# The fullest expert's 96 slots as three products of 32 columns instead of 64 + 32

## The chip, the core and the metric

The kernel runs on one core of a Trainium2 chip. The metric is the device time of one execution in microseconds: 2082.15 us is the median of three runs before the change (2079.93 to 2087.93). One further execution was profiled, and all rows below come from it.

## What is computed

The reference is a two-layer backbone block for a diffusion generator: 256 latent and 256 context tokens of width 1024. Layer 0 mixes the sequence with a bidirectional state-space scan, layer 1 with bidirectional retention. Each layer ends in a mixture of 32 experts, of which every token takes two from one group of eight. This part is what the change touches:

```python
def expert_block(args):
    xb, e = args
    gu = xb @ w_gate_up[e]                       # 1024 -> 2 x 512
    return (jax.nn.silu(gu[:, :MOE_HIDDEN]) * gu[:, MOE_HIDDEN:]) @ w_down[e]   # 512 -> 1024
...
return jnp.sum(out[dest].reshape(n_tok, MOE_TOP_K, -1) * top_w[..., None], axis=1)
```

Layer 0 routes 512 tokens (context and latent), layer 1 the 256 latent ones. All arithmetic is in f32.

## The kernel before

**Slots and places.** The router sorts the experts by their number of tokens (a few by fixed position), and the table `SLOTS` gives each position a number of slots, 32, 64 or 96. One position per layer, number 4, has 96. `MoE.__init__` puts positions together into *places* of 128 slots: two experts of 64, four of 32, or the *full* place, which is position 4 (96 slots) and one partner with 32. Layer 0 has twelve places, of which the full one is the fourth; layer 1 has ten, and it is the second.

**One place.** The tokens of a place's slots stand in `xT` as eight slabs of 128 features by 128 slots. `gate_up` (L1810) runs over eight slabs `k`, and in each over two halves: gate into the PSUM bank `pg`, up into `pu`. In every half each expert multiplies: its slot columns of `xT` are the stationary operand (so an expert with 32 slots uses 32 columns of TensorE's array and 32 partitions of the result), and 512 columns of its weights stream through. `hidden_T` turns the activated result (L1827, `ph`), `down` (L1839) does four slabs of two halves in the same way into `pd`, `weighted` scales and splits it, and `add` brings it back to the tokens with a one-hot matrix (L1857, `pc`; L1882 and L1883 on VectorE). I call one half of one slab a *step*: a place has 16 gate/up steps and 8 down steps, whatever its kind. Which products a step has is set by `tiles_of` (L1501): a list of pairs (expert, width), used by `pairs`, by `gate_up` and `down` through `parts`, and by `slot_w` (L1769), where VectorE reduces one row per tile.

For the full place `tiles_of` gives widths 64, 32 and 32: the expert at position 4 multiplies twice per step, with slots 0 to 63 on columns 0 to 63 and slots 64 to 95 on columns 64 to 95, both times with the same streamed weights; the partner has columns 96 to 127.

**The one-hot rows.** `scatter_oh` (L1780) spreads each tile's token positions over its columns with a small bf16 product per tile (`pb`), all with the same streamed operand `posT`. It compares them with a column of slot numbers, which `pairs` picks by the widths: 0 to 31 repeated for four experts, 0 to 63 repeated for two, 0 to 95 for the full place.

**The weight stream.** An expert's weights are six loads of 1 MB: four for gate and up (two slabs each), two for down. The ring (`Ring`) issues all loads of both layers in one order from SP's queue (L175): place by place, and within a place load 0 of each expert, then load 1. It has 16 slots of 1 MB in layer 0 and 19 in layer 1, in five kinds named A, B, E, F and X. A load waits in SP's queue until the product that last read its slot is done, and all loads behind it wait too.

**The order on TensorE.** The program is written place by place, but a scheduler orders each engine's instructions. It mixes gatherings of a later place (`px`, L1749), the one-hot sums (`pc`) and weights (`pw`) into the steps, and it may move the partner's products away from those of position 4. What it has placed is fixed when the kernel is built.

Of the kernel before, what the change touches and what calls it, by code (L numbers as in the profile page):

```python
# [198 lines left out]
def col(S, name, a=0, b=None):  # L199
    o, w = CL[name]  # L200
    return S.c[:, o + a:o + (w if b is None else b)]
# [1272 lines left out]
class MoE:  # L1474
# [25 lines left out]

    def tiles_of(self, places):  # L1501

        return [(e, w) for e in places for w in ([64, 32] if self.slots(e) == 96 else [self.slots(e)])]

    def slots(self, e):
        return SLOTS[self.layer][e]
# [379 lines left out]
    def pairs(self):  # L1886
        S, order, groups = self.S, self.order, self.groups
        i96, s32, s64, s96 = (col(S, n) for n in ("i96", "s32", "s64", "s96"))
        xT, ws, G = {}, {}, self.G
        last = len(order) - 1  # L1890

        def one_hots(g):
            runs = []
            for e in (e for p in groups[g] for e in order[p]):
                if runs and e == runs[-1][1] and self.slots(e) == self.slots(runs[-1][0]):
                    runs[-1][1] += 1
                else:
                    runs.append([e, e + 1])
            return self.gather_oh([(self.pos[:, :, a:b], self.slots(a)) for a, b in runs], i96)

        def weights(g):
            for j, p in enumerate(groups[g]):
                ws[p] = self.slot_w(G[g], P * j, order[p])

        def start(g):
            for p in groups[g]:
                xT[p] = self.wk.tile([P, 8, P], F32, name="xT", bufs=3)

        def part(g, q, nb=2):
            self.gather(G[g], [xT[p] for p in groups[g]], q, nb)  # L1910

        def ahead(p, g):
            own = groups[g - 1]
            for q in range(4)[slice(4 * own.index(p) // len(own), 4 * (own.index(p) + 1) // len(own))]:
                part(g, q)
            if p == own[-1]:
                weights(g)
        start(0)
        prev = None
        later = self.rest_of_route()  # L1920

        def first(k):
            if k < 2 or k % 2 == 0:
                part(0, k if k < 2 else k // 2, 1 if k < 2 else 2)
            if k in ROUTE_K:
                next(later)

        def after(th, W, os_, w, end=False):
            nonlocal prev
            hT = self.hidden_T(th)  # L1930
            if prev is not None:
                self.add(*prev)
            pd = self.down(W, hT)
            prev = (os_, pd, w) if end else (os_, self.weighted(pd, w), 2)
        for p, places in enumerate(order):
            g = next(j for j, own in enumerate(groups) if p in own) + 1
            new = g < len(groups) and p == groups[g - 1][0]
            experts = {e: Expert(S, self.layer, e) for e in places}
            tiles = self.tiles_of(places)
            W = [(experts[e], w) for e, w in tiles]  # L1940
            if new and p:
                G[g] = one_hots(g)
            th = self.gate_up(W, xT[p], None if p else first)
            if p == 0:
                G[1] = one_hots(1)
                self.spread_rows()
            widths = [w for _, w in tiles]
            os_ = self.scatter_oh([(S.id2[:, e:e + 1], w) for e, w in tiles],
                                  s32 if widths[0] == 32 else s64 if widths[1] == 64 else s96)
            if g < len(groups):  # L1950
                if p == 0:
                    weights(0)
                    self.blocks()
                    self.base()
                if new:
                    start(g)
                if p > LATE:
                    ahead(p, g)
            after(th, W, os_, ws[p], p == last)
            if g < len(groups) and p <= LATE:  # L1960
                ahead(p, g)
            if p == REST[self.layer]:
                self.add(*prev)
                prev = None
                self.rest()
        return prev
# [287 lines left out]
```

## Time and profile before

| what | value |
|---|---|
| median of three runs | 2082.15 us |
| profiled execution, own time | 2085.92 us |
| its span, first to last instruction | 2084.1 us |
| granted TensorE clock, mean | 0.950 |
| first mixer (0 to 648 us) | PE busy 553.52, stream 144 GB/s |
| experts of layer 0 (648 to 1190) | PE busy 506.01, stream 363 GB/s |
| retention (1190 to 1584) | PE busy 337.07, stream 174 GB/s |
| experts of layer 1 (1584 to 2084) | PE busy 432.36, stream 371 GB/s |

Times count from the span's start. The *stream* is what the DMA engines moved, nearly all of it weights. In the two expert stages both TensorE and the stream are busy most of the time, so which of them a stretch waits for has to be read from that stretch. A row such as `pg<-ringB,xT 128*64 128x512` is a product that writes `pg`, with a stationary operand of 128 by 64 from `xT` and 512 streamed columns of a weight slot of kind B. The timeline joins instructions that follow one another, and names a joined row by its first one.

### The profile page before, as it was taken

The numbers are of one execution on the slowest core, as the hardware profiler recorded it, in microseconds if no ns is written. First come the engines' busy times: TensorE is split into PE (matmuls) and PEld (weight loads), VectorE is DVE, ScalarE is ACT, GpSimd is POOL, SyncE is SP. The second block draws the span as 40 slices with busy tenths as digits, with TensorE's granted clock in tenths as the row PEclk, the third lists the DMA queues.
The fourth block names the chain that finished last, engine by engine and source line by source line (L and its number), as shares of the span: only waits on it lengthen the run. The fifth ranks groups of instructions, "written<-read, shape, count | busy, mean of one in ns | idle before, by whom it ended". The sixth has DMA issues, their size and how long they took to land. (4 is left out here: it accounts for less than half of the span.)

```text
span 2084.1 us, 24190 instructions
## 1 busy us (share of the span) xinstructions
PE 1829.0 (88%) x9251; PEld 1038.1 (50%) x9251; DVE 1010.0 (48%) x1755; ACT 503.8 (24%) x879; POOL 517.6 (25%) x332
## 2 busy tenths in 40 slices
PE   7798889889986999999998879888897999878886
PEld 4576657567674432333332368776873233223221
DVE  3868687877576432251432475664444333103112
ACT  2655454554212100000000143232232001000000
POOL 1454645454335000000000053364551100000000
PEclk9899999999996999999999989999997999999999
DMA  7332322234845997699998844455467969999996
GB/s 292 109 122 81 129 104 101 102 131 151 282 156 202 365 395 310 249 417 382 414 403 352 333 162 162 165 199 176 130 237 299 409 253 409 409 378 407 409 409 254
DMA packets 137947, 544.42 MB, mean 261 GB/s; under 512 B 10369, under 2 KB 10881, under 8 KB 125153
## 3 DMA queue, kind: packets, MB, share of 16 engines
q1 hardware_dynamic: 137392, 542.59, 67.8%
q8 instruction: 75, 1.23, 0.2%
q14 instruction: 48, 0.39, 0.1%
q10 hardware_dynamic: 432, 0.21, 0.0%
HBM read 537.52 MB, written 5.24 MB: 260 GB/s over the span
## 5 line engine op out<-in xcount | busy, mean ns | idle before, releaser
L430 POOL TENSOR_TENSOR wl<-ringA,wh 128x1024 fp32r<-128x1024 f32 x117 | 295.3, 2539 | 808.2 <-ACT wh L429 800.4
L429 ACT ACTIVATE wh<-ringA 128x1024 fp32r<-128x1024 f32 x120 | 126.1, 1058 | 193.5 <-issue 45.3
L1839 PE MATMUL pd<-ringB,hT 128*32 128x512 f32 (+1 forms) x448 | 143.2, 640 | 5.8 <-ACT hT L1829 4.1
L1850 DVE SCALAR_TENSOR_TENSOR yh<-pd,ws,yh 128x512 fp32r<-128x512 f32 x40 | 30.0, 751 | 206.5 <-ACT yh L1849 204.9
L1819 DVE SCALAR_TENSOR_TENSOR th<-th,pg 128x512 f32<-128x512 f32 x22 | 15.1, 687 | 222.5 <-ACT th L1815 222.5
L1815 ACT ACTIVATE th<-pg 128x512 f32<-128x512 f32 x22 | 13.1, 597 | 432.7 <-PE pg L1810 422.6
L1810 PE MATMUL pg<-ringE,xT 128*32 128x512 f32 (+1 forms) x308 | 110.8, 611 | 7.9 <-DMA ringE<-in_moe_w_gate_up_dram 7.4
L2114 POOL TENSOR_TENSOR oacc<-oacc,ringX 128x512 f32<-128x512 f32 x1 | 1.6, 1623 | 452.2 <-ACT oacc L196 452.2
L1810 PE MATMUL pu<-ringE,xT 128*32 128x512 f32 (+1 forms) x308 | 111.0, 615 | 2.5 <-DMA ringE<-in_moe_w_gate_up_dram 2.5
L1882 DVE TENSOR_TENSOR tl<-pc,ringB 128x512 f32<-128x512 f32 x124 | 80.9, 685 | 44.6 <-PE pc L1857 43.0
L1810 PE MATMUL pg<-ringB,xT 128*32 128x512 f32 (+1 forms) x260 | 94.5, 620 | 7.2 <-DMA ringB<-in_moe_w_gate_up_dram 7.2
L1173 PE MATMUL pin<-u,wh 128*128 128x256 f32 (+1 forms) x256 | 84.1, 329 | 16.7 <-DVE gT L1225 11.3
L726 DVE SCALAR_TENSOR_TENSOR cacc<-pad,cw,cacc 128x512 f32<-128x512 f32 x96 | 94.5, 987 | 7.0 <-ACT cacc L724 6.3
L1810 PE MATMUL pu<-ringB,xT 128*32 128x512 f32 (+1 forms) x260 | 93.7, 616 | 0.1
L1810 PE MATMUL pg<-ringA,xT 128*32 128x512 f32 (+1 forms) x232 | 87.1, 603 | 6.4 <-DMA ringA<-in_moe_w_gate_up_dram 5.9
L1749 PEld LDWEIGHTS px<-oh,hhl 128*128 128x128 f32 x576 | 73.3, 193 | 35.6 <-issue 33.2
L1857 PE MATMUL pc<-yh,os 128*128 128x512 f32 x248 | 82.5, 432 | 8.5 <-DVE tl L1882 8.0
L1810 PE MATMUL pu<-ringA,xT 128*32 128x512 f32 (+1 forms) x232 | 86.4, 608 | 1.8 <-DMA ringA<-in_moe_w_gate_up_dram 1.8
L1839 PE MATMUL pd<-ringE,hT 128*32 128x512 f32 (+1 forms) x232 | 80.9, 614 | 7.4 <-DMA ringE<-in_moe_w_down_dram 4.5
L969 POOL TENSOR_TENSOR cd<-cb,tokv 128x512 f32<-128x512 f32 x64 | 73.2, 1144 | 46.2 <-DVE W L973 25.4
L1749 PE MATMUL px<-oh,hhl 128*128 128x256 f32 (+1 forms) x576 | 83.2, 294 | 0.0
L1174 PE MATMUL pin<-u,wh 128*128 128x256 f32 (+1 forms) x256 | 82.5, 322 | 0.1
(403 smaller groups left out, 4326.4 us busy)
## 6 DMA issues: line engine op xcount, KB each, us to landing
ringE<-in_moe_w_gate_up_dram SPq DMA_DIRECT2D x76, 1024.0 KB, 18.0
ringB<-in_moe_w_gate_up_dram SPq DMA_DIRECT2D x63, 1024.0 KB, 16.6
ringA<-in_moe_w_gate_up_dram SPq DMA_DIRECT2D x55, 1024.0 KB, 15.1
ringB<-in_moe_w_down_dram SPq DMA_DIRECT2D x53, 1024.0 KB, 18.0
ringA<-in_mod_w_dram SPq DMA_DIRECT2D x40, 1024.0 KB, 5.0
ringF<-in_moe_w_gate_up_dram SPq DMA_DIRECT2D x34, 1024.0 KB, 17.6
ringX<-in_moe_w_gate_up_dram SPq DMA_DIRECT2D x28, 1024.0 KB, 17.4
ringE<-in_moe_w_down_dram SPq DMA_DIRECT2D x28, 1024.0 KB, 18.1
```

Source lines behind the costliest of these rows:

```text
L429: S.split = nc.scalar.activation(hi, w, AF.Copy).ins
L430: (eng or nc.gpsimd).tensor_tensor(lo, w, hi.bitcast(F32), OP.subtract)
L726: nc.vector.scalar_tensor_tensor(acc, pad[:, :, t:t + 256], cw[:, m, t:t + 1], acc, op0=OP.mult, op1=OP.add)
L969: G.tensor_tensor(cd[d], cb[:, d, c, None, :].to_broadcast([P, 4, 128]), tokv[:, c, 0, o:o + 4, None].to_broadcast([P, 4, 128]), OP.mult)
L1173: self.S.nc.tensor.matmul(p, a, self.uh(k)[:, T], start=k == 0, stop=False)
L1174: self.S.nc.tensor.matmul(p, a, self.ul(k)[:, T], start=False, stop=False)
L1749: nc.tensor.matmul(px[:, b, :], self.S.hhl[i][:, m, j * 128:(j + 1) * 128], oh[:, i], start=i == 0 and m == 0, stop=i == nt - 1 and m == 1)
L1810: nc.tensor.matmul(po[o:o + n, :], xT[:, k, a:a + n], w.get(k)[:, u * 512:(u + 1) * 512], start=k == 0, stop=k == 7)
L1839: nc.tensor.matmul(pd[u % n][o:o + m, :], hT[:, j, a:a + m], w.get(8 + j)[:, u * 512:(u + 1) * 512], start=j == 0, stop=j == 3)
L1850: self.S.nc.vector.scalar_tensor_tensor(yl[:, u], p, ws, yh[:, u].bitcast(F32), op0=OP.mult, op1=OP.subtract)
L1857: self.S.nc.tensor.matmul(pc, os_[s, i * 128:(i + 1) * 128], ys[q][s, u % n], start=q == 0, stop=q == 1)
L1882: V.tensor_tensor(t, pc, self.gate(i)[:, c], OP.mult)
```

## The change

For the full place, the expert at position 4 gets three tiles of 32 slots where it had one of 64 and one of 32. With the partner, a step then has four products of 32 columns. Since the first width is now 32 in this place too, the choice of the slot-number column is made by the number of experts.

```diff
     def tiles_of(self, places):
-        return [(e, w) for e in places for w in ([64, 32] if self.slots(e) == 96 else [self.slots(e)])]
+
+        return [(e, w) for e in places for w in ([32] * 3 if self.slots(e) == 96 else [self.slots(e)])]
...
             os_ = self.scatter_oh([(S.id2[:, e:e + 1], w) for e, w in tiles],
-                                  s32 if widths[0] == 32 else s64 if widths[1] == 64 else s96)
+                                  s64 if widths[0] == 64 else s32 if len(experts) == 4 else s96)
```

The numbers of slots, the grouping into places, the order of the loads and the results are the same. From L1503 on, lines move down by one.

On TensorE, the end of the gate/up steps of layer 0's full place, before (`ringB` is a slot with weights; rows of 64 and of 32 columns belong to position 4, a single row of 32 at the start of a pair to the partner):

```order
L1810 MATMUL pg<-ringB,xT 64x512
L1810 MATMUL pg<-ringB,xT 32x512
L1810 MATMUL pu<-ringB,xT 64x512
L1810 MATMUL pu<-ringB,xT 32x512
L1810 MATMUL pg<-ringB,xT 32x512
L1810 MATMUL pu<-ringB,xT 32x512
L1810 MATMUL pg<-ringB,xT 64x512
L1810 MATMUL pg<-ringB,xT 32x512 x2
L1810 MATMUL pu<-ringB,xT 64x512
L1810 MATMUL pu<-ringB,xT 32x512 x2
L1827 MATMUL ph<-c,th 128x128 x4
```

And the same stretch after the change:

```order
L1811 MATMUL pg<-ringB,xT 32x512 x3
L1811 MATMUL pu<-ringB,xT 32x512 x3
L1811 MATMUL pg<-ringB,xT 32x512
L1811 MATMUL pu<-ringB,xT 32x512
L1811 MATMUL pg<-ringB,xT 32x512 x4
L1811 MATMUL pu<-ringB,xT 32x512 x4
L1828 MATMUL ph<-c,th 128x128 x4
```

Nothing changes its place: each pair 64 and 32 becomes three of 32, and where the partner stood apart it still does.

On TensorE, the end of the down steps of the same place, before (`px` is the gathering for a later place, `ringX` a slot with the partner's weights):

```order
L1749 MATMUL px<-oh,hhl 128x256 x11
L1839 MATMUL pd<-ringX,hT 32x512 x2
L1839 MATMUL pd<-ringB,hT 64x512
L1839 MATMUL pd<-ringB,hT 32x512
L1839 MATMUL pd<-ringX,hT 32x512
L1839 MATMUL pd<-ringB,hT 64x512
L1839 MATMUL pd<-ringB,hT 32x512
L1839 MATMUL pd<-ringX,hT 32x512
L1749 MATMUL px<-oh,hhl 128x256 x7
```

After the change:

```order
L1750 MATMUL px<-oh,hhl 128x256 x11
L1840 MATMUL pd<-ringX,hT 32x512 x2
L1840 MATMUL pd<-ringB,hT 32x512 x3
L1840 MATMUL pd<-ringX,hT 32x512
L1840 MATMUL pd<-ringB,hT 32x512 x3
L1840 MATMUL pd<-ringX,hT 32x512
L1750 MATMUL px<-oh,hhl 128x256 x8
```

Again the products stay where they were; one product of a gathering moved behind the last down step.

On TensorE, the first gate/up steps of layer 1's full place, before:

```order
L1810 MATMUL pu<-ringX,xT 32x512 x2
L1810 MATMUL pg<-ringX,xT 64x512
L1810 MATMUL pg<-ringX,xT 32x512 x2
L1810 MATMUL pu<-ringX,xT 64x512
L1810 MATMUL pu<-ringX,xT 32x512 x2
L1810 MATMUL pg<-ringA,xT 64x512
```

After the change:

```order
L1811 MATMUL pu<-ringX,xT 32x512 x3
L1811 MATMUL pg<-ringX,xT 32x512 x4
L1811 MATMUL pu<-ringX,xT 32x512 x4
L1811 MATMUL pg<-ringA,xT 32x512 x4
```

Here the partner's product stands in the same row as the three others in nearly every step. SP's, ScalarE's and GpSimd's instructions keep their order; on VectorE the full place has one more reduction in `slot_w`, and a few additions near it trade places.

## Prediction

> **What bounds the kernel now.** I read the page first, for the engines' shares and for the slices of the whole span.
>
> ```profile
> PE 1829.0 (88%) x9251; PEld 1038.1 (50%) x9251; DVE 1010.0 (48%) x1755; ACT 503.8 (24%) x879; POOL 517.6 (25%) x332
> ...
> DMA  7332322234845997699998844455467969999996
> GB/s 292 109 122 81 129 104 101 102 131 151 282 156 202 365 395 310 249 417 382 414 403 352 333 162 162 165 199 176 130 237 299 409 253 409 409 378 407 409 409 254
> ```
>
> TensorE is busy nearly everywhere, so its share says little by itself. The slices of 52.1 us say more: in the two expert stages (slices 13 to 22 and 31 to 39) the weight stream runs at 380 to 417 GB/s, with one hole in each, slices 15 and 16 (310 and 249) and slice 32 (253). I looked up what runs there: it is the one place per layer that the change touches. The busy time of the gate and up products (L1810) and then of the down products (L1839), by stretch, gives its price. The columns are the stretch, its length, PE busy (records), PEld busy (records), the clock, the DMA share and GB/s.
>
> ```profile
> 783.00:826.00 43.00, 37.38 (x96) 6.47 (x96) 1.00 0.80 314
> ...
> 851.00:875.00 24.00, 17.76 (x128) 5.81 (x128) 1.00 0.71 268
> ...
> 1629.00:1667.00 38.00, 33.85 (x96) 5.70 (x96) 1.00 1.03 409
> ...
> 1690.00:1713.00 23.00, 17.76 (x128) 5.80 (x128) 1.00 0.71 268
> ```
>
> ```profile
> 826.00:851.00 25.00, 19.80 (x48) 3.37 (x48) 1.00 0.44 166
> ...
> 875.00:894.00 19.00, 10.88 (x64) 2.86 (x64) 1.00 1.02 414
> ...
> 1667.00:1690.00 23.00, 17.91 (x48) 3.02 (x48) 1.00 0.52 196
> ...
> 1713.00:1733.00 20.00, 12.52 (x64) 3.15 (x64) 0.91 1.03 408
> ```
>
> The first and third rows of each fence are the full place of layer 0 and of layer 1, the second and fourth the place of four experts right behind it. Both kinds have 16 gate/up steps and 8 down steps. The place of four issues more records (128 against 96) and takes half the time. The reason stands in the timeline of PE: start, length, instructions.
>
> ```profile
> 820.55 2.05 PE L1810 MATMUL pg<-ringB,xT 128*64 128x512 f32 x6
> ...
> 821.55 1.05 PE L1810 MATMUL pg<-ringB,xT 128*32 128x512 f32 x4
> 822.53 2.05 PE L1810 MATMUL pu<-ringB,xT 128*64 128x512 f32 x6
> ...
> 868.54 1.11 PE L1810 MATMUL pg<-ringB,xT 128*32 128x512 f32 x8
> 869.40 1.11 PE L1810 MATMUL pu<-ringB,xT 128*32 128x512 f32 x8
> ```
>
> One step of the full place lasts 822.53 - 820.55 = 1.98 us: first the product on 64 columns alone, and 1.00 us later, when it has left, the two on 32 columns side by side. (A product of f32 is two records.) One step of the four-expert place lasts 869.40 - 868.54 = 0.86 us, with four products of 32 columns side by side. So products of one width overlap, and products of two widths don't.
>
> Who sets the pace around these places? The weight stream in four stretches, and what SP, which issues it, waits for in the hole of layer 0 (783 to 870) and then of layer 1 (1630 to 1707):
>
> ```profile
> 805.00:868.00 63.00, 61.03 (x244) 17.72 (x246) 13.47 (x21) 3.34 (x6) 0.00 (x0) 1.00 0.52 192
> 877.00:950.00 73.00, 68.46 (x309) 27.66 (x305) 28.24 (x53) 5.31 (x9) 0.00 (x0) 1.00 1.03 415
> ...
> 1672.00:1707.00 35.00, 34.43 (x166) 10.64 (x167) 12.05 (x28) 2.14 (x4) 0.00 (x0) 1.00 0.49 179
> 1707.00:2064.00 357.00, 306.14 (x1388) 97.74 (x1381) 66.94 (x123) 26.17 (x46) 0.00 (x0) 0.98 1.01 402
> ```
>
> ```profile
> SPq L175 <- PE pu L1810: 51.8, 9, 11.6
> SPq L175 <- PE pd L1839: 23.0, 2, 11.6
> ```
>
> ```profile
> SPq L175 <- PE pu L1810: 37.6, 8, 10.7
> SPq L175 <- PE pd L1839: 21.1, 2, 12.0
> ```
>
> The stream stands still because all ring slots hold weights that the full place hasn't used: TensorE sets the pace there, and each slot it holds longer is a load issued later. Behind the holes the layers differ. In layer 0, TensorE's waits for loads behind the place (851 to 1190) are small:
>
> ```profile
> PE pg L1810 <- DMA ringB<-in_moe_w_gate_up_dram: 2.2, 2, 1.4
> PE pg L1810 <- DMA ringA<-in_moe_w_gate_up_dram: 2.0, 1, 2.0
> PE pd L1839 <- DMA ringB<-in_moe_w_down_dram: 1.6, 3, 0.6
> ```
>
> In layer 1 the stream runs full from 1707 to 2064, and the last of the chain of waits is one load behind the other:
>
> ```profile
> 2024.34 18.49 DMA ringE<-in_moe_w_gate_up_dram
> ...
> 2044.83 18.41 DMA ringE<-in_moe_w_down_dram
> 2063.28 2.78 PE pd L1839 x18
> ```
>
> So layer 0's end moves with TensorE, and layer 1's end moves with the stream.
>
> **The change part by part.** *Layer 0.* Every step of the full place becomes four products of one width, as in the place behind it, so I price it by that place: 37.38 + 19.80 = 57.18 us become 17.76 + 10.88 = 28.64, which saves 28.5. By steps it is 24 x (1.98 - 0.86) = 26.9; the rest are partner products that today run alone, between other work. All of it is on the path: PE is busy 61.03 of the 63 us in the hole. Can the loads follow? Against the rate behind the hole, the stream lost 63 x (1 - 192/415) = 33.9 us, more than the 28.5 that TensorE wins; the loads for the next places are issued when slots come free, and these come free earlier by the same time. What could be late next is the small waits for loads just quoted; with 33.9 against 28.5 they don't grow. Layer 0 gives 28.5. Ends: 33.9 (the stream's whole loss), and half, 14, if loads become what is waited for.
>
> *Layer 1.* By the same comparison 33.85 + 17.91 = 51.76 becomes 17.76 + 12.52 = 30.28, 21.5 less (the four-expert place has a gathering in the middle of its down half, so this is the low side; 24 steps by 1.12 give 26.9). But the end is set by the stream, which lost 35 x (1 - 179/402) = 19.4 us. TensorE's gain is larger than the hole, so the hole closes, and no more than the hole is won; the other 2 to 7 us turn into waiting for loads. Layer 1 gives 19.4. The low end is half, 9.7, if slots still come free too late for a stream without gaps.
>
> *More instructions.* Per layer 16 + 8 products of the experts and one of the one-hot rows, each with its weight load. They lie under the other columns: the four-expert place has the same four per step, its loads fill 5.81 us of PEld under 17.76 of PE. The one-hot rows (L1780) even get shorter. Here are three products of two widths (with a row label of the first), and four of one width; in both, all read the same streamed operand:
>
> ```profile
> 764.28 0.72 PE L1780 MATMUL pb<-posT,id 64*64 64x512 bf16 x3
> ```
>
> ```profile
> 735.46 0.40 PE L1780 MATMUL pb<-posT,id 64*32 64x512 bf16 x4
> ```
>
> That is 0.3 us less per layer, counted at nothing. On DVE one more reduction per layer (L1770) is some 0.2 us, while DVE waits for TensorE:
>
> ```profile
> L1770 DVE TENSOR_REDUCE ws<-pw x66: 136/157/168, 686.9 to 1973.2; 32x1 f32<-32x2 f32 x44, 64x1 f32<-64x2 f32 x22
> ```
>
> SP's loads keep their order, so no queue is rearranged. Retention between the layers only starts earlier.
>
> *A rule against it.* The row of four one-hot products is done in the time of one, so I count four columns as full overlap. The Trainium skill (TensorE: Matmul & The Clock Gate, Part 3, Measured speedup vs the span model) gives 2.38x for three column tiles, not 3x. By that figure a step would take an estimated 0.86 x 3 / 2.38 = 1.08 us, the saving would shrink by 24 x 0.22 = 5.3 us a layer, and the sum would be about 40 instead of 48. No row here shows such a loss, and the steps of 0.86 with four columns speak against it.
>
> *The sum.* 28.5 + 19.4 = 47.9 us. The profiled execution took 2085.92 us (span 2084.1 and 1.8 around it), so it would take 2038.0. It lies 3.8 us above the median of 2082.15; on the median the forecast is 2034.
>
> **The rivals.**
> 1. *The loads give part of it back.* In layer 0 loads become what is waited for, or in layer 1 slots come free in lumps and the stream keeps gaps. For it: the small DMA waits in layer 0, and today's issues in lumps of two to eight. Against it: the stream's loss is larger than TensorE's gain in layer 0, and smaller in layer 1. Half of either layer lost gives 2044 to 2048, half of both 2034 + 24 = 2058.
> 2. *The partner's product runs alone.* The order puts the fourth column's product behind the three instead of beside them; a step is 2 x 0.86 = 1.72, the saving 24 x 0.26 x 2 = 12.5, the time 2070. Against it: most of the new rows hold four products in one run, and four-expert places with such splits still take 17.76.
> 3. *Nothing moves*, because the stream needs its time anyway: 2082. Against it: the stream idles for half of each hole, and SP's waits there name TensorE.
> 4. *Slower.* The three products of one expert read the same streamed weights; were they to run one behind the other, a step would be 3 x 0.86 = 2.58 (the partner's beside one of them), 0.60 more than 1.98, on the path in both holes: 48 x 0.60 = 28.8, the time 2111. It decides as soon as a step takes over 1.98. Against it: the row of four one-hot products with one streamed operand, 0.40 us together.
>
> **How the numbers follow.** The forecast of 2034 has a chance of 0.72, rival 1 0.15, rival 2 0.05, rival 3 0.04, rival 4 0.04. The lower end of the range takes 33.9 + 19.4 = 53.3 and the spread of the runs below the median (2.2): 2082.15 - 55.5 = 2026. The upper end is rival 1 with both halves, 2058. Together that holds 0.87; rivals 2 to 4 are left out. A measurement of this kernel can tell about 0.5% (10 us) from no change. Faster by more: 0.72 + 0.15 + 0.05 = 0.92; within: 0.04; slower: 0.04.
>
> **What would show it.** Right: in both full places no record of 64 columns, steps of 0.86 us, some 28 us for the 24 steps; slices of the stream without the two holes; layer 0's stage about 28 us shorter, layer 1's about 19, with more waits of PE for loads behind its full place. Wrong: steps above 1.1 us (the rule or rivals 2 and 4), holes that stay while the steps are short (rival 1), or both stages shortened in TensorE's busy time and not in length (rival 3).

## The result, and the profile after

The changed kernel takes 2033.07 us (median of 4 runs, 2030.15 to 2037.89), against 2083.16 (4 runs) for the kernel before on the same chip: a ratio of 0.976 with an interval of 0.9732 to 0.9789. The forecast was 2034. The profiled execution took 2031.26 us, its span is 2029.5, and its mean clock is 0.948 (0.950 before), so the two executions can be laid side by side.

First the page of the kernel after: shares of the engines, then the DMA share and GB/s of 40 slices, of 50.7 us now.

```profile
PE 1776.5 (88%) x9349; PEld 1031.8 (51%) x9349; DVE 1007.5 (50%) x1757; ACT 504.2 (25%) x879; POOL 517.9 (26%) x332
...
DMA  7322323242863899899999944464457999999996
GB/s 298 114 107 101 114 84 145 84 156 89 262 233 131 308 392 408 352 417 381 414 410 370 363 166 145 151 245 155 138 216 296 409 409 409 409 374 408 409 409 251
```

TensorE issues 98 records more and is busy 52.5 us less. The hole of layer 0 (310 and 249 before) is left as one slice of 352, and the hole of layer 1 (253) is gone: slices 31 to 34 read 409. Nothing else in the line changed much (slices are counted from 0, as in the prediction); TensorE's share is the same 88%, which says as little now as it did before.

Next the same stretches as in the prediction, gate/up products (L1811) and then down products (L1840): the full place and the four-expert place of layer 0, then the two of layer 1. Columns: stretch, length, PE busy (records), PEld busy (records), clock, DMA share, GB/s.

```profile
785.00:808.00 23.00, 17.94 (x128) 4.73 (x128) 1.00 1.02 413
...
827.00:851.00 24.00, 17.76 (x128) 5.81 (x128) 1.00 0.72 281
...
1594.00:1615.00 21.00, 16.23 (x128) 4.21 (x128) 1.00 1.03 409
...
1629.00:1650.00 21.00, 16.82 (x127) 5.52 (x125) 1.00 1.03 409
```

```profile
808.00:827.00 19.00, 12.70 (x64) 2.71 (x64) 0.91 1.02 417
...
851.00:870.00 19.00, 10.87 (x64) 2.86 (x64) 1.00 1.03 415
...
1615.00:1630.00 15.00, 8.11 (x64) 2.10 (x64) 1.00 1.03 409
...
1650.00:1670.00 20.00, 13.95 (x64) 3.26 (x64) 0.91 1.03 408
```

The full place of layer 0 is down from 57.18 us of products to 17.94 + 12.70 = 30.64, that of layer 1 from 51.76 to 16.23 + 8.11 = 24.34. The stream runs at 409 to 417 GB/s through both of them; during their down products it ran at 166 and 196 before.

How a step looks now, in the timeline of PE (start, length, instructions), first with the partner beside the three products on the same weights, then two rows later in the place:

```profile
796.48 1.07 PE L1811 MATMUL pg<-ringF,xT 128*32 128x512 f32 x8
797.36 1.06 PE L1811 MATMUL pu<-ringF,xT 128*32 128x512 f32 x8
...
803.37 1.07 PE L1811 MATMUL pg<-ringB,xT 128*32 128x512 f32 x8
804.23 1.07 PE L1811 MATMUL pu<-ringB,xT 128*32 128x512 f32 x8
```

Eight records are four products of f32, and the next step starts 0.86 to 0.88 us later, where a step took 1.98. That three of the four read the same streamed operand makes no difference.

Where the time came from shows in the ends of the stages. Here are the products that turn the hidden rows (`ph`) in the first place of layer 0, its last place, and the first place of layer 1, each with the times from first to last; first of before, then of after.

```profile
L1827 PE MATMUL ph<-c,th x4: 272/273/327, 688.1 to 688.5; 128*128 128x128 f32 x4
...
L1827 PE MATMUL ph<-c,th x4: 272/272/329, 1174.1 to 1174.5; 128*128 128x128 f32 x4
...
L1827 PE MATMUL ph<-c,th x4: 421/421/475, 1616.3 to 1617.0; 128*128 128x128 f32 x4
```

```profile
L1828 PE MATMUL ph<-c,th x4: 272/272/330, 689.9 to 690.3; 128*128 128x128 f32 x4
...
L1828 PE MATMUL ph<-c,th x4: 272/273/328, 1146.6 to 1147.0; 128*128 128x128 f32 x4
...
L1828 PE MATMUL ph<-c,th x4: 421/421/474, 1581.4 to 1582.1; 128*128 128x128 f32 x4
```

From the first to the last of layer 0 it is 486.0 us before and 456.7 after; from there to layer 1, the stage of retention, 442.2 and 434.8; from there to the end of the span, 467.8 and 448.1. That is 29.3, 7.4 and 19.7 us. The middle one is a surprise, since the change touches nothing there; the section on the hardware comes back to it. The same three marks are used for every run below: "layer 0", "retention" and "layer 1" are these lengths.

In layer 1 the gain is first larger and then partly given back. Against before, the same instruction comes 34.9 us earlier at the first of the marks in layer 1, some 63 us earlier at the `ph` row of the place behind the full one (1714.0 in before, 1650.5 in after), and 54.7 at the end. Of the 28 us that were won in between, some 9 were lost again in waits for loads at the places behind. The stream from the full place to the end, and the longest of TensorE's waits for loads there (us, times, longest):

```profile
1594.00:1672.00 78.00, 75.57 (x504) 30.02 (x502) 25.82 (x61) 8.70 (x18) 0.00 (x0) 0.98 1.03 409
1653.00:2010.00 357.00, 306.46 (x1341) 95.19 (x1340) 65.07 (x120) 25.00 (x44) 0.00 (x0) 0.97 1.01 401
```

```profile
PE pg L1811 <- DMA ringE<-in_moe_w_gate_up_dram: 7.0, 10, 1.5
PE pd L1840 <- DMA ringE<-in_moe_w_down_dram: 4.9, 8, 0.7
PE pg L1811 <- DMA ringA<-in_moe_w_gate_up_dram: 4.7, 5, 1.5
```

The chain of waits still ends with load behind load, and 2 us of products between them, as it did before:

```profile
1969.70 18.47 DMA ringE<-in_moe_w_gate_up_dram
...
1990.15 18.41 DMA ringE<-in_moe_w_down_dram
```

So the end of layer 1 belongs to the stream in both kernels, and it came earlier by as much as the stream lost in its hole.

### The profile page after: what moved, and what is told of

It is laid out like the page before. It is cut to its first block, busy times and chain, and to the rows that moved or that the text cites. A ratio compares the mean times of both kernels' runs of the same rounds, so it can differ in the third digit from the quotient of the medians.

```text
span 2029.5 us, 24390 instructions
## 1 busy us (share of the span) xinstructions
PE 1776.5 (88%) x9349; PEld 1031.8 (51%) x9349; DVE 1007.5 (50%) x1757; ACT 504.2 (25%) x879; POOL 517.9 (26%) x332
## 5 line engine op out<-in xcount | busy, mean ns | idle before, releaser
L1840 PE MATMUL pd<-ringB,hT 128*32 128x512 f32 (+1 forms) x472 | 125.3, 640 | 5.3 <-ACT hT L1830 4.5
L1811 PE MATMUL pg<-ringE,xT 128*32 128x512 f32 (+1 forms) x312 | 110.3, 618 | 7.4 <-DMA ringE<-in_moe_w_gate_up_dram 7.0
L1811 PE MATMUL pu<-ringE,xT 128*32 128x512 f32 (+1 forms) x312 | 110.1, 619 | 3.6 <-DMA ringE<-in_moe_w_gate_up_dram 3.6
L1811 PE MATMUL pg<-ringB,xT 128*32 128x512 f32 (+1 forms) x268 | 89.4, 610 | 6.0 <-DMA ringB<-in_moe_w_gate_up_dram 6.0
L1811 PE MATMUL pg<-ringA,xT 128*32 128x512 f32 (+1 forms) x244 | 84.6, 609 | 5.2 <-DMA ringA<-in_moe_w_gate_up_dram 4.7
L1811 PE MATMUL pu<-ringB,xT 128*32 128x512 f32 (+1 forms) x268 | 87.9, 602 | 0.1
L1811 PE MATMUL pu<-ringA,xT 128*32 128x512 f32 (+1 forms) x244 | 84.2, 618 | 2.8 <-DMA ringA<-in_moe_w_gate_up_dram 2.8
L1840 PE MATMUL pd<-ringE,hT 128*32 128x512 f32 (+1 forms) x240 | 78.3, 607 | 7.8 <-DMA ringE<-in_moe_w_down_dram 4.9
```

The source lines that it names most:

```text
L1811: nc.tensor.matmul(po[o:o + n, :], xT[:, k, a:a + n], w.get(k)[:, u * 512:(u + 1) * 512], start=k == 0, stop=k == 7)
L1840: nc.tensor.matmul(pd[u % n][o:o + m, :], hT[:, j, a:a + m], w.get(8 + j)[:, u * 512:(u + 1) * 512], start=j == 0, stop=j == 3)
```

## The experiments

The theory is the prediction's: a step of two widths costs 1.98 us because the product on 64 columns runs alone; with one width it costs 0.86; layer 0 takes all that TensorE wins, layer 1 no more than its stream lost. Rival theories were that the loads of layer 0 reach into layer 1 (or give part back), that the change of width on the array is what costs, and that the gains of gate/up and down simply add. All of these kernels compute the whole reference. The three lengths of each profiled execution, in us, and the time of the runs with the ratio to the kernel before on the same chip (2083.16 us for after; 2083.57 for the four kernels that change one layer or one half, 2083.93 for the last two):

| kernel | layer 0 | retention | layer 1 | median | ratio (interval) |
|---|---|---|---|---|---|
| before | 486.0 | 442.2 | 467.8 | | |
| after | 456.7 | 434.8 | 448.1 | 2033.07 | 0.976 (0.9732 to 0.9789) |
| layer 0 alone | 458.3 | 435.7 | 468.3 | 2053.42 | 0.9861 (0.9835 to 0.9887) |
| layer 1 alone | 484.6 | 438.2 | 448.4 | 2062.65 | 0.9908 (0.9883 to 0.9933) |
| gate/up alone | 465.8 | 439.2 | 449.2 | 2045.91 | 0.9822 (0.9798 to 0.9846) |
| down alone | 479.8 | 437.9 | 460.0 | 2067.94 | 0.9925 (0.9901 to 0.995) |
| widths grouped | 482.1 | 436.8 | 463.0 | 2074.41 | 0.9961 (0.9942 to 0.9979) |
| all products on 32 | 455.7 | 440.0 | 448.0 | 2031.70 | 0.9749 (0.9712 to 0.9786) |

### The change in one layer alone

The edit is to `tiles_of`; the constant for the scatter's one-hot rows is chosen to fit the number of tiles.

```diff
-        return [(e, w) for e in places for w in ([64, 32] if self.slots(e) == 96 else [self.slots(e)])]
+        return [(e, w) for e in places for w in (([32] * 3 if self.layer == 0 else [64, 32]) if self.slots(e) == 96 else [self.slots(e)])]
```

The second kernel has `self.layer == 1` in that line. What was expected of them, of layer 0 and then of layer 1:

> Three products of 32 in layer 0 alone. Theory (products of two widths don't overlap; in layer 0 TensorE sets the pace, so what it wins reaches the end): 24 steps of 0.86 us there, layer 0 some 26 to 31 us shorter, layer 1 as before; 2052 to 2057 us. Rival (only layer 1's end, set by the weight stream, counts): within 10 us of 2083.

> Three products of 32 in layer 1 alone. Theory (TensorE wins some 27 us in the place, the stream's hole of 19.4 us is all that reaches the end): layer 1 18 to 20 us shorter, 2062 to 2066 us. Rival (all that TensorE wins reaches the end): 26 to 28 us shorter, 2055 to 2057 us.

Measured: 2053.42 and 2062.65 us, gains of about 30 and 21. In the profiled executions the change in layer 0 shortens layer 0 by 27.7 us and leaves layer 1 at 468.3; in layer 1 it shortens layer 1 by 19.4. The GB/s lines of the two pages, layer 0 alone first:

```profile
GB/s 294 113 110 96 113 95 132 83 154 123 252 202 155 343 389 409 353 415 381 416 402 363 333 145 142 155 257 149 101 266 337 400 257 409 409 378 407 409 409 251
```

```profile
GB/s 296 110 118 88 114 105 120 83 154 123 275 178 184 361 390 332 219 415 381 415 415 349 403 166 159 151 212 167 154 163 297 408 409 409 409 374 407 409 409 252
```

Each closes its own hole and leaves the other (slice 32 at 257 in the first, slices 15 and 16 at 332 and 219 in the second). Nothing passes from one layer to the other, and the cap in layer 1 is there when it is changed alone: a rival that let TensorE's whole gain through had expected 2055 to 2057.

### The change in one half of the place alone

Here only the gate/up steps, or only the down steps, of the full place use three products of 32; everything else keeps 64 and 32.

```diff
+            W3 = [(experts[e], v) for e, w in tiles for v in ([32] * (w // 32) if FULL in places else [w])]
-            th = self.gate_up(W, xT[p], None if p else first)
+            th = self.gate_up(W3, xT[p], None if p else first)
```

```diff
-            after(th, W, os_, ws[p], p == last)
+            after(th, W3, os_, ws[p], p == last)
```

Expected, gate/up first:

> Three products of 32 in the gate/up steps of both layers; the down steps and the one-hot rows keep 64 and 32. Theory: layer 0 gains 18 to 20 us, layer 1 nearly all of its 17 us, since that is below the hole of 19.4: 35 to 38 us in all, 2045 to 2048 us. Rival (a fixed share of TensorE's gain is lost in layer 1, about 0.7 of it arrives): layer 1 gains 12 us.

> Three products of 32 in the down steps of both layers alone. Theory: layer 0 gains 8 to 10 us, layer 1 all of its 9 to 10 us: 17 to 20 us in all, 2063 to 2066 us. With the gate/up run, layer 1's two parts then add up to some 26 us where both together give 19.5: the hole caps the sum. Rival (a fixed share of 0.7 arrives): layer 1 gains 7 us, and the parts add up to what both together give.

Measured: 2045.91 and 2067.94 us. The first is as expected; the second misses its interval by 2. In layer 0 the halves give 20.2 and 6.2 us, together 26.4 against the 27.7 of layer 0 alone. In layer 1 they give 18.6 and 7.8, together 26.4 against 19.4 of layer 1 alone: there the gains don't add, and it is the hole that they run into. (The medians alone are too coarse for this: the halves gain 37.7 and 15.6 us, together 53.3, against 50.1 for both, and each ratio's interval is some 5 us wide to either side. The stage lengths carry it: layer 1 took 448.0 to 448.4 us in the three executions with both halves changed, and 467.8 and 468.3 in the two with neither.) The stream shows it. With gate/up alone, it is full across layer 1's place and the places behind it; with down alone, more than half of the hole remains (50 x (1 - 314/402) = 10.9 us of the 19.4). First the kernel with gate/up alone, then the one with down alone:

```profile
1640.00:1720.00 80.00, 75.69 (x391) 28.27 (x387) 20.65 (x42) 7.07 (x13) 0.00 (x0) 1.00 1.02 406
```

```profile
1660.00:1710.00 50.00, 47.84 (x319) 19.81 (x321) 16.88 (x37) 5.47 (x11) 0.00 (x0) 1.00 0.81 314
```

Gate/up's 16 steps alone bring 18.6 of the possible 19.4 us, so that the down steps have next to nothing left to win there. The shortfall of the down half in layer 0 (6.2 for an expected 8 to 10) does not lie in the place: over the place itself the shift against before is 8.8 us (from 2.5 late to 6.3 early). Some 2.6 of it are lost again by the layer's end, 1.6 of them at the second place behind it, where this execution has a stretch of half clock at 912.8 that before doesn't have (more of this below); the last microsecond stays open.

### Both widths kept, sorted by width

If it is the missing overlap that costs, two steps with the two 64-wide products first and then the 32-wide ones still take four turns; they save only some of the four changes of width. A rival said that a change of width costs about a product by itself (1.1 us).

```diff
-            for u, po in ((0, pg), (1, pu)):
-                for o, n, w, a in self.parts(W, u):
-                    nc.tensor.matmul(...)
+            for width in (64, 32):
+                for u, po in ((0, pg), (1, pu)):
+                    for o, n, w, a in self.parts(W, u):
+                        if n == width:
+                            nc.tensor.matmul(...)
```

The down products are sorted the same way.

> The kernel before, with the products of a slab in another order: the 64-wide ones of both halves first, then the 32-wide ones of both halves, so that the width changes half as often with the same products. Theory (what costs is that products of two widths don't overlap, the change itself only some 0.13 us each): two steps take 3.7 us instead of 3.96, the place gains 3 to 4 us per layer; 2075 to 2078 us. Rival (the change of width itself costs, some 1.1 us for each step's pair of changes): two steps take 2.8 us, the place gains 13 us per layer; 2060 to 2064 us.

Measured: 2074.41 us over 10 runs, a ratio of 0.9961; layer 0 is 3.9 us shorter and layer 1 4.8, a little more than expected. The timeline of PE in layer 0's full place:

```profile
814.87 1.07 PE L1812 MATMUL pg<-ringB,xT 128*64 128x512 f32 x2
815.77 1.02 PE L1812 MATMUL pu<-ringB,xT 128*64 128x512 f32 x2
816.73 1.06 PE L1812 MATMUL pg<-ringB,xT 128*32 128x512 f32 x4
817.61 1.03 PE L1812 MATMUL pu<-ringB,xT 128*32 128x512 f32 x4
818.57 1.07 PE L1812 MATMUL pg<-ringB,xT 128*64 128x512 f32 x2
```

Two steps take 818.57 - 814.87 = 3.70 us where two mixed ones took 2 x 1.98 = 3.96. Four turns of 0.86 would be 3.44, so the 3.70 contain two changes at 0.13 each; the four changes of the mixed order cost 3.96 - 3.44 = 0.52, again 0.13 each. The width change is thus a small part of the 1.12 us that a step lost; the rest, 0.86, is a turn of TensorE spent on 64 of the columns. The Trainium skill (TensorEngine Tiling (Array Packing), Key Properties) says that changing the tiling mode drains TensorE, and gives no price. These rows agree: products on the two sides of a change don't overlap, and that is the dear part; the 0.13 us come on top.

### Every product on 32 columns

Ten places hold two experts with 64 slots each, two products of 64 side by side. If one width is what counts, four of 32 there are as good as two of 64.

```diff
-        return [(e, w) for e in places for w in ([64, 32] if self.slots(e) == 96 else [self.slots(e)])]
+        return [(e, 32) for e in places for _ in range(self.slots(e) // 32)]
```

> The changed kernel with products of 32 columns in every place: the experts of 64 slots multiply twice as well, which adds 24 x 2 products with their weight loads to each of the 7 + 3 places of two experts. Theory (only the change of width costs, and four products cost what two of 64 do): steps of those places stay at 0.86 us, 2030 to 2038 us, as the changed kernel. Rival (every added product or weight load costs issue time, some 0.05 us): 24 x 2 x 10 x 0.05 = 24 us more, 2057 us. Rival (narrow products are faster by themselves): the steps of places of two fall below 0.8 us and the time below 2025.

Measured: 2031.70 us, ratio 0.9749, with layers of 455.7 and 448.0 us: the same as after within the spread. In a place of two, the steps begin every 0.86 us, as in before (702.41 and 703.27 there); rows of PE, the fourth product being among the rows left out:

```profile
702.09 0.60 PE L1810 MATMUL pg<-ringE,xT 128*32 128x512 f32 x2
...
702.95 0.60 PE L1810 MATMUL pu<-ringE,xT 128*32 128x512 f32 x2
...
703.80 0.60 PE L1810 MATMUL pg<-ringE,xT 128*32 128x512 f32 x2
```

Twice the products and weight loads in ten places cost nothing that shows. It is also no gain: these places had one width already. No kernel tried here beats the changed one by more than its runs spread.

## Why the prediction was right

**The step.** 0.86 us was forecast, from the four-expert place, and 0.86 to 0.88 was measured. The figure that the prediction weighed against it, 2.38x for three column tiles by the Trainium skill (TensorE: Matmul & The Clock Gate, Part 3, Measured speedup vs the span model), with an estimated step of 1.08, is not borne out here: four products of 512 columns of f32 take the time of one.

**Layer 0's term, 28.5 us.** The place now has 30.64 us of products and not 28.64. The term was too large by about two, and it is the down half: 12.70 us in place of 10.88. One row carries nearly all of it, the first down row of the place:

```profile
809.71 3.54 PE L1840 MATMUL pd<-ringB,hT 128*32 128x512 f32 x12 [0.42 <-ACT hT L1830]
813.18 0.50 PE L1750 MATMUL px<-oh,hhl 128*128 128x256 f32 x2
```

These are two steps, which should take 1.7 us and take 3.47. The granted clock of the stretch says why: 0.50 for 3.4 us.

```profile
809.60:813.00 3.40, 3.29 (x12) 0.57 (x12) 0.49 (x1) 0.06 (x1) 0.00 (x0) 0.50 1.02 408
```

This is no accident of one execution: the same stretch, behind the `ph` row of this place, is in all four traces whose gate/up steps there are four products of 32 (after, layer 0 alone, gate/up alone, all on 32), and in none of the other four. From its first gate/up product to that of the next place, the full place takes 827.65 - 785.20 = 42.45 us, 26.0 less than before; without this stretch it would be 27.7. By the layer's end the difference is 29.3, though. It grew by 1.6 and 1.7 us at two places where before has such a stretch and after hasn't, at 1053.4 and at 1097.8 in the trace of before:

```profile
1053.40:1056.80 3.40, 3.40 (x7) 0.92 (x7) 0.00 (x0) 0.00 (x0) 0.00 (x0) 0.50 1.02 419
...
1097.80:1101.20 3.40, 3.40 (x12) 0.97 (x10) 0.00 (x0) 0.00 (x0) 0.00 (x0) 0.50 1.04 424
```

With layer 0 alone it is 26.0 at the place too, and the second of these stretches brings it to 27.7. So the lengths of 29.3 and 27.7 stand on either side of 28.5, but the place itself gave 2.5 us less than the term says: a stretch of half clock that the prediction didn't count took 1.7 of them, and where half clock fell in the execution of before gave as much back, or more. That the term came out so closely is luck in this part; its mechanism, and all but these 2.5 us of its size, are not.

**Do the loads follow in layer 0?** Yes. The prediction set the stream's loss of 33.9 us against TensorE's 28.5, and expected a stream that keeps up with something to spare. It does: in the DMA view, in slices of 2.5 us from 783, only three slices (21, and the two beside it) are near empty.

```profile
GB/s 401 416 413 415 415 419 413 406 411 413 406 410 410 419 419 428 419 421 419 300 23 7 46 413 413 415 413 408 408 403 419 419 419 419 421 419 424 419 421 418
```

What is left of the hole, about 8 us of it, is the part that TensorE's gain didn't reach, of the size that 33.9 - 26 suggests. SP's longest waits there still name TensorE (785 to 850), 46.3 us together where the two rows of the prediction had 74.8 (783 to 870):

```profile
SPq L175 <- PE pu L1811: 30.0, 13, 12.3
SPq L175 <- PE pd L1840: 16.3, 4, 8.9
```

**Layer 1's term, 19.4 us.** 19.7 in the profiled pair and 19.4 with layer 1 alone. TensorE won 51.76 - 24.34 = 27.4 us at the place, a little above the 21.5 to 26.9 named, and the stream's hole capped what remained of it, as forecast. That gate/up alone already gives 18.6, and that the halves sum to 26.4, shows the cap from a second side.

**Counted at nothing**, and so measured: the weight loads of the added products (twice as many in ten further places cost nothing). The one-hot rows and the added reduction, 0.3 and 0.2 us by the prediction, are too small for these runs to show.

**The rivals.** Loads giving part back is seen in layer 1 alone (some 9 of 28 us), where it was in the sum already. The partner's product alone (a step of 1.72), nothing moving, and one product behind the other (a step of 2.58) are out by the step of 0.86. The sum of 47.9 us stands against 50.1 between the medians and 54.7 between the two profiled executions; of the latter, 7.4 came from a stage that the change doesn't touch. The interval of the ratio allows 44 to 56 us, so the microsecond between the forecast of 2034 and the median is partly luck.

## What to carry to other kernels

Products on different columns of TensorE's array overlap when they have one width, and here not at all when they have two; count a step in turns, one for each change of width, and cut an expert's slots so that all products of a step are equally wide, even if it takes more of them. Price a place by a neighbour that already has the form it is to get, and check the gain against what the weight stream lost beside it: where the stream sets the end of the stage, that loss is all there is to win. When two parts are undone one by one and their gains sum to more than both together, there is such a cap between them.

## What the runs showed of the hardware

Two things were not expected. The granted clock drops to 0.50 in 30 to 34 stretches of an execution, most of them 3.4 or 6.8 us long and a few longer, and a stretch of 3.4 us costs 1.7 us where TensorE is the bound. In each trace all changes of the clock lie on one grid of 3.41 us, and what TensorE did in the window ahead of a drop tells where one comes. Here are two windows of that grid in after, at the end of the gate/up steps of layer 0's full place and of the place behind it (columns: stretch, length, PE busy, PEld, DVE, ACT and POOL busy, clock, DMA share, GB/s):

```profile
806.19:809.60 3.41, 1.75 (x10) 0.52 (x8) 1.63 (x3) 1.09 (x2) 0.00 (x0) 1.00 1.04 412
850.57:853.98 3.41, 2.32 (x14) 0.92 (x14) 1.61 (x3) 0.60 (x1) 0.00 (x0) 1.00 1.03 408
```

In both, TensorE pauses for VectorE and ScalarE around the `ph` row. In the first it was busy for 51% of the window, and the stretch of half clock at 809.6 follows; in the second for 68%, and none follows. The two expert stages of all eight traces, from the first to the last `ph` row of each layer, go the same way. Of the windows at full clock, 39 had TensorE busy for less than 45%, and half clock follows all of them; 65 had 45 to 55%, and it follows 34; 1895 had more, and it follows none. So where TensorE is busy at half clock, it is the window before that held little work. That this is the cause is not shown, since no run changed these pauses alone. The Trainium skill (TensorE: Matmul & The Clock Gate, Part 1, What's actually happening) describes a gate with half rate and windows of 3413 ns. The 3.4 us and the 0.50 agree.

Some stretches also differ between executions of the same instructions: in the first mixer, which no kernel here changes, six traces have one at 431 to 433 us, and before and all on 32 have none. Partly for that reason a stage whose instructions are the same in all eight profiled executions (but for a few products at its ends with all on 32) took between 434.8 and 442.2 us. Half clock lasts 61.8 us of the shortest, that of after, but 68.0 of the longest, that of before, and 73.0 of the 440.0 with all on 32, so the clock alone doesn't put them in order, and the rest stays open. The two executions of before and after happen to have the two ends of this spread. A difference of a few us between single profiled executions of this kernel is therefore not a finding, unless the traces show where it arose; the last microsecond of the down half in layer 0, and that by which layer 0 of the all-32 kernel is shorter, are left at that.
